# Six chain steps in place of four per block of projection products, in the last chunk of tokens

## The chip, the cores and the metric

The kernel runs on one core of a Trainium2 chip. The metric is the device time of one execution in microseconds (us); smaller is better. Before the change the median of three runs is 2636.89 us (2636.56 to 2642.58).

## The reference

One encoder layer over 2048 tokens of width 1024, all float32. Cut to what matters here:

```python
h = rmsnorm(x, norm1_g)
qa, ka, va, qm, km, vm, om, gm, mg = split_cols(h @ w_in, IN_SPLITS)
ya = windowed_gqa(qa, ka, va, ...)          # 8 heads, window of 128 to each side, softmax with a sink
ym = mlstm_branch(qm, km, vm, om, gm, ...)  # conv, a scan over the tokens forward and one backward, norm, gate om
g = sigmoid(mg + merge_b)
x = x + (g[:, :D] * (ya @ w_branch_attn) + g[:, D:] * (ym @ w_branch_mlstm)) @ w_out
x = x + hier_moe(rmsnorm(x, norm2_g), ...)  # 32 experts, two per token
```

## The kernel before, in words

Every float32 product is made as three products of a high and a low part (hi·hi, hi·lo, lo·hi), so each weight piece is split into `whi` (ACT, L236) and `wlo` (POOL or DVE, L239) after its load into `wraw` (SP, L220).

**First phase.** The tokens go in four chunks of 512 (0 to 3), each of four blocks of 128 tokens (the last chunk has blocks 12 to 15). For each chunk a list of pieces of `w_in` is worked off: keys, values and gates, then queries, the recurrence's inputs, its output gate `o`, and the eight merge pieces `mg`. All these products are line L319 on `hThi`/`hTlo`, called projection products here. A result of `mg` or `o` is drawn out of PSUM by ACT and stored (`mg_s` L912, `o_s`).

**Chains.** The other work of this phase is written as generators that are advanced a step at a time: attention of a block (`attn`: turned queries L505, scores L524/L525, their sum with the bias L527, maximum L529, `exp` L536, turned probabilities L545, product with the values L556, the turned reciprocal L572, result `yT` L578, stored to `ya_s` L579), the recurrence (`mhead`: L678 to L709, `mtile`: L732 to L765) and its closing part (`mpost_load`, `mpost`: gate load `og` from `o_s` L782, gate scaling L798, sum of the two directions L790, square and its sum L793/L795, root on POOL L197/L198, L800, L801, turning L805, copy L814, store to `ym_s` L815). `run_mms` issues the products of a group and after every 12 narrow or 6 wide ones (a block) takes `tick_n[0]` steps round robin over the chains. Up to the last chunk that is 2; in the last chunk, once the recurrence's inputs are all there (`qkv_done`), it is `TL`. The last chunk's queue of steps holds the forward recurrence to block 15, the attention of blocks 12 to 15, and the backward recurrence of blocks 15 to 12, pushed when `o` is through. A step that finds its chain empty is no step.

**Order.** The order in which the program writes the steps is not the order of the queues: outside the parts marked as a manual schedule, a list scheduler with its own timeline puts the instructions on the five engines' queues; each queue then runs strictly in its order. What the program writes earlier has the earlier place where several are ready.

**Second phase.** For chunks 3 down to 0: attention and recurrence results are loaded, multiplied by the branch weights (L319 on `yahi`, `yalo`, `ymhi`, `ymlo`: branch products), weighted (L1151 to L1156), multiplied by `w_out` (L319 on `uhi`, `ulo`, added to x in L1163), normed and routed, while the backward recurrence of the next chunk runs as a chain. For chunk 3 `yprep_first` does the loading, after all chains of the chunk are through: into `ulo` from `ya_s` and `ym_s` (SP, L1137), then `yahi`/`ymhi` by ACT (L1138), `yalo`/`ymlo` by DVE (L1139). `gprep` (turns L591, scan L605, L613, L614) prepares the gates of the next chunk's backward recurrence. **Third phase:** the experts, in a manual schedule.

Of the kernel before, what the change touches and what calls it, by code (L numbers as in the profile page):

```python
# [102 lines left out]
def body(tc, A, out, scr_ext=None, upto="all"):  # L103
    nc = tc.nc
    scr_ext = scr_ext or {}
    es = ExitStack()
    with es:
        pass
        _body(tc, nc, A, out, scr_ext, upto, es)


def _body(tc, nc, A, out, scr_ext, upto, es):
# [211 lines left out]
                ch.tick(tick_n[0])  # L324

    tick_n = [2]
    TL = 4


    Fes = ExitStack()  # L330
# [586 lines left out]
    def qkv_done(c):  # L917
# [4 lines left out]
        if c == NCH - 1:  # L922
            tick_n[0] = TL
        ch.drain("cv")
# [926 lines left out]
```

## Time and profile before

| | |
|---|---|
| median of the runs | 2636.89 us |
| profiled execution, own time | 2630.14 us |
| its span, first to last instruction | 2628.4 us |
| PE / DVE / ACT / POOL busy, share of the span | 94 / 61 / 49 / 35 % |
| last projection product ends at | 1210.24 us |
| first branch product starts at | 1236.36 us |
| first turn of the experts' inputs starts at | 1784.65 us |

PE is TensorE, PEld its weight loads, DVE VectorE, ACT ScalarE, POOL GpSimd, SP the queue that issues most transfers. Times in the trace count from the span's start. Matmuls overlap in the pipeline, so that a wide product lasts 0.40 us by the profile while the next starts 0.23 us after it.

### The profile page before, as it was taken

Reading aid. Unit: us, or ns where it says so; the run is one execution under the profiler, and the core shown is the slowest. Engines: PE = TensorE matmul, PEld = TensorE weight load, DVE = VectorE, ACT = ScalarE, POOL = GpSimd, SP = SyncE. Lnnn points to the kernel's source line nnn. Section 1 sums busy time; section 2 is a strip of 40 time slices with the busy share of each in tenths; the row PEclk is TensorE's granted clock in tenths of the full one; section 3 lists DMA queues with packets and bytes.
Section 4 is the critical chain, followed back from the end, with each engine's and each line's share of the span. In section 5 each row is a group of like instructions: output and inputs, shape, how many; then the busy total and the mean of one; then the engine's idle time right before and its main releaser. Section 6 shows DMA issues by size and latency. Waiting matters only on the chain. (4 is left out here: it accounts for less than half of the span.)

```text
span 2628.4 us, 39004 instructions
## 1 busy us (share of the span) xinstructions
PE 2474.8 (94%) x13932; PEld 2070.8 (79%) x13933; DVE 1613.8 (61%) x2687; ACT 1285.4 (49%) x2516; POOL 928.6 (35%) x918
## 2 busy tenths in 40 slices
PE   7999999999999999997898898988999999999997
PEld 7777987889778978875787887886777777777776
DVE  4454535544554655555858495767877676678765
ACT  4444545454544544443334242325766565667654
POOL 5443444334433433242544454532222111112111
PEclk9999999999999999998999998998999999999999
DMA  4534533453344534556777573639998797989974
GB/s 151 160 118 144 161 94 120 130 172 116 114 124 125 161 113 139 160 154 195 219 216 213 157 226 102 207 111 330 334 360 267 256 330 240 294 256 361 365 245 101
DMA packets 348411, 515.31 MB, mean 196 GB/s; under 512 B 25019, under 2 KB 212500, under 8 KB 348188
## 3 DMA queue, kind: packets, MB, share of 16 engines
q1 hardware_dynamic: 332140, 460.03, 53.4%
q0 software_dynamic: 14880, 48.20, 7.8%
q10 hardware_dynamic: 1168, 4.21, 0.4%
q8 instruction: 127, 2.08, 0.3%
q14 instruction: 96, 0.79, 0.1%
HBM read 420.83 MB, written 91.54 MB: 195 GB/s over the span
## 5 line engine op out<-in xcount | busy, mean ns | idle before, releaser
L239 POOL TENSOR_TENSOR wlo<-wraw,whi 128x512 fp32r<-128x512 f32 (+1 forms) x422 | 573.5, 1386 | 476.9 <-ACT whi L236 455.6
L1563 DVE TENSOR_TENSOR elo<-raw,ehi 128x1024 fp32r<-128x1024 f32 x256 | 299.4, 1220 | 26.3 <-ACT ehi L1562 26.3
L319 PE MATMUL mm<-hThi,whi 128*128 128x512 f32 x768 | 306.9, 400 | 0.0
L319 PE MATMUL mm<-hTlo,whi 128*128 128x512 f32 x768 | 304.4, 396 | 0.0
L319 PE MATMUL mm<-hThi,wlo 128*128 128x512 f32 x768 | 304.0, 396 | 0.0
L236 ACT ACTIVATE whi<-wraw 128x512 fp32r<-128x512 f32 (+1 forms) x424 | 233.4, 622 | 141.5 <-PE mm L319 67.5
L319 PE MATMUL mm<-whi,hThi 128*128 128x256 f32 (+1 forms) x896 | 261.2, 292 | 4.0 <-ACT ev L898 1.8
L1562 ACT ACTIVATE ehi<-raw 128x1024 fp32r<-128x1024 f32 x256 | 254.5, 1050 | 19.7 <-DMA raw<-w_expert_up 19.1
L319 PE MATMUL mm<-wlo,hThi 128*128 128x256 f32 (+1 forms) x896 | 256.9, 287 | 1.1 <-POOL wlo L239 1.1
L319 PE MATMUL mm<-whi,hTlo 128*128 128x256 f32 (+1 forms) x896 | 256.5, 286 | 0.0
L1677 POOL DMA_INDIRECT out<-y,idx x32 | 56.2, 1756 | 445.0 <-DVE y L1676 226.2
L1609 PE MATMUL mm<-ehi,xhi 128*128 128x512 f32 x512 | 205.2, 401 | 0.0
L1609 PE MATMUL mm<-ehi,xlo 128*128 128x512 f32 x512 | 200.7, 392 | 0.6 <-DVE xlo L1588 0.6
L319 PEld LDWEIGHTS mm<-whi,hThi 128*128 128x128 f32 x896 | 171.0, 191 | 8.1 <-ACT ev L898 2.1
L319 PEld LDWEIGHTS mm<-wlo,hThi 128*128 128x128 f32 x896 | 171.2, 191 | 3.4 <-issue 1.6
L319 PEld LDWEIGHTS mm<-whi,hTlo 128*128 128x128 f32 x896 | 171.0, 191 | 0.3 <-DVE hTlo L444 0.2
L319 PEld LDWEIGHTS mm<-hThi,wlo 128*128 128x128 f32 x768 | 144.3, 188 | 33.9 <-issue 3.2
L319 PEld LDWEIGHTS mm<-hThi,whi 128*128 128x128 f32 x768 | 144.6, 188 | 29.3
L319 PEld LDWEIGHTS mm<-hTlo,whi 128*128 128x128 f32 x768 | 144.5, 188 | 28.6
L319 PE MATMUL mm<-whi,uhi 128*128 128x256 f32 x448 | 134.0, 300 | 26.4 <-DVE x L1163 20.4
L1612 PE MATMUL mm<-elo,xhi 128*128 128x512 f32 x512 | 158.5, 391 | 0.0
L1563 DVE TENSOR_TENSOR elo<-rawd,ehi 128x1024 fp32r<-128x1024 f32 x128 | 151.5, 1221 | 10.9 <-ACT ehi L1562 10.4
(438 smaller groups left out, 5830.1 us busy)
## 6 DMA issues: line engine op xcount, KB each, us to landing
wraw<-w_in SPq DMA_DIRECT2D x152, 512.0 KB, 4.2
raw<-w_expert_gate SPq DMA_DIRECT2D x128, 512.0 KB, 9.2
raw<-w_expert_up SPq DMA_DIRECT2D x128, 512.0 KB, 10.4
rawd<-w_expert_down SPq DMA_DIRECT2D x64, 1024.0 KB, 11.5
mg_s<-evg SPq DMA_DIRECT2D x64, 256.0 KB, 3.1
gt<-mg_s SPq DMA_DIRECT2D x32, 512.0 KB, 6.0
wraw<-w_out SPq DMA_DIRECT2D x32, 512.0 KB, 6.2
xt<-x SPq DMA_DIRECT2D x16, 512.0 KB, 4.6
```

What stands on the lines that cost most here:

```text
L236: nc.scalar.activation(hi[:, ks, :W], r[:, k:k + 2, :W], AF.Copy)
L239: eng.tensor_sub(lo[:, ks, :W], r[:, k:k + 2, :W], hi[:, ks, :W].bitcast(F32))
L319: nc.tensor.matmul(o, l, r, start=st, stop=sp)
L1562: nc.scalar.activation(dst[0], src, AF.Copy)
L1563: nc.vector.tensor_tensor(dst[1], src, dst[0].bitcast(F32), op=OP.subtract)
L1609: nc.tensor.matmul(self.gu[h], x_[:, k % 4, :], self.wt(k)[0][:, h, :], start=k == 0 and i == 0, stop=False)
L1612: nc.tensor.matmul(self.gu[h], self.xs[k // 4][0][:, k % 4, :], self.wt(k)[1][:, h, :], start=False, stop=k == KT - 1)
L1677: nc.gpsimd.indirect_dma_start(out=out, out_offset=bass.IndirectOffsetOnAxis(ap=self.idx, axis=0), in_=y, in_offset=None, compute_op=OP.add)
```

## The change

One number: the steps that are taken after each block of the last chunk's products, from the point on where the recurrence's inputs are complete.

```diff
     tick_n = [2]
-    TL = 4
+    TL = 6
```

The steps themselves stay the same (some 260 of them are taken from that point to the end of the first phase in both). As written, they are through in the fourth merge piece before and in the second now. The scheduler turns this into other queue orders from there on, up to the third phase.

PE's queue where the first phase ends. Before, this is all that stands between the last projection product and the first branch product (T, O and rb belong to the attention of block 15, mw and mib to the recurrence of blocks 13 and 12, LF, gz and mrow to `gprep`):

```order
L545 MATMUL T<-ident,sc 128x128 x2
L805 MATMUL m<-ident,mw 128x128 x4
L545 MATMUL T<-ident,sc 128x128 x2
L758 MATMUL m<-mv_11210,mib 128x129 x2
L545 MATMUL T<-ident,sc 128x128 x4
L758 MATMUL m<-mv_11210,mib 128x129 x2
L572 MATMUL T<-ident,rb 128x128 x4
L556 MATMUL O<-PT,vv 64x512 x2
L805 MATMUL m<-ident,mw 128x128 x4
L591 MATMUL m<-ident,LF 4x128 x4
L591 MATMUL m<-ident,gz 4x128 x4
L613 MATMUL m<-ident,mrow 128x4 x4
```

Now the last projection product, what follows it, and the first branch products:

```order
L319 MATMUL mm<-hThi,wlo 128x512
L805 MATMUL m<-ident,mw 128x128 x4
L758 MATMUL m<-mv_11353,mib 128x129 x4
L805 MATMUL m<-ident,mw 128x128 x4
L591 MATMUL m<-ident,LF 4x128 x4
L591 MATMUL m<-ident,gz 4x128 x4
L613 MATMUL m<-ident,mrow 128x4 x4
L614 MATMUL m<-D_12126,ones_91 128x16
L678 MATMUL m<-ident,MM 128x128 x4
L319 MATMUL mm<-yahi,whi 128x512 x2
```

The eight turns of probabilities, the four turns of the reciprocal and the two rows of value products have moved ahead of the last 16 projection products; L614 and L678, which stood 20 and 36 branch products further on, have moved ahead of the first one.

DVE's queue at the gate scaling of block 12, before:

```order
L801 TENSOR_TENSOR mw<-mw,og 128x512
L527 TENSOR_TENSOR sc<-S,bias 128x256 x3
L529 TENSOR_REDUCE mx<-sc 128x4
L798 SCALAR_TENSOR_TENSOR og<-og,ogain 128x512
L531 TENSOR_TENSOR mx<-mx,sinkb 128x4
L748 TENSOR_TENSOR mdn<-mdn,EN 128x2
L532 TENSOR_SCALAR nmx<-mx 128x4
```

and now:

```order
L765 SCALAR_TENSOR_TENSOR Cst<-Cst,mil,m 128x129 x2
L801 TENSOR_TENSOR mw<-mw,og 128x512
L551 COPY PT<-T 128x512
L798 SCALAR_TENSOR_TENSOR og<-og,ogain 128x512
L748 TENSOR_TENSOR mdn<-mdn,EN 128x2
L749 RECIPROCAL mdn<-mdn 128x2
L750 TENSOR_TENSOR mw<-m,mdn 128x256
L578 TENSOR_TENSOR yT<-O,PT 128x512
```

The maximum of block 15's scores (L529 to L532) no longer straddles the gate scaling; it stands ahead of L801.

SP's queue at the loads of the branch inputs, before:

```order
L815 DMA ym_s<-hf 128x4x128
L220 DMA wraw<-w_branch_mlstm 128x4x256
L579 DMA ya_s<-yT 128x4x128
L220 DMA wraw<-w_branch_attn 64x4x256 x2
L1137 DMA ulo<-ya_s 128x4x128 x4
L1137 DMA ulo<-ym_s 128x4x128 x3
L1145 DMA gt<-mg_s 128x2x512
```

and now:

```order
L579 DMA ya_s<-yT 128x4x128
L656 DMA mw<-st_s 128x512
L658 DMA mv_12198<-v_s 128x4x128
L912 DMA mg_s<-evg 128x512
L815 DMA ym_s<-hf 128x4x128
L220 DMA wraw<-w_branch_mlstm 128x4x256
L782 DMA og<-o_s 128x512
L1137 DMA ulo<-ya_s 128x4x128 x3
L815 DMA ym_s<-hf 128x4x128
L1137 DMA ulo<-ya_s 128x4x128
```

The gate load for the next chunk (L782), which came after the loads of the branch inputs, now stands ahead of them, and one store of the closing part has come between them.

## Rows read from the trace of the kernel before

**Rows 1.** Busy time by stretches: stretch, length, PE, PEld, DVE, ACT, POOL, clock, DMA, GB/s.

```profile
1010.00:1020.00 10.00, 7.62 (x53) 7.42 (x52) 3.87 (x6) 2.29 (x5) 3.90 (x5) 0.83 0.73 231
...
1015.00:1195.00 180.00, 180.00 (x1042) 146.16 (x1042) 102.49 (x211) 86.68 (x229) 56.85 (x59) 1.00 0.50 154
...
1230.00:1240.00 10.00, 5.17 (x17) 3.60 (x18) 6.28 (x12) 4.79 (x8) 0.00 (x0) 0.50 1.16 310
...
1270.00:1280.00 10.00, 8.71 (x42) 6.85 (x40) 9.70 (x18) 2.48 (x5) 3.71 (x6) 1.00 1.01 333
```

**Rows 2.** PE's waits from 1195 to 1260 us: total, times, longest (us).

```profile
PE m L591 <- ACT hf L814: 4.5, 1, 4.5
PE T L572 <- DVE rb L568: 3.3, 1, 3.3
PE T L545 <- ACT sc L536: 3.1, 1, 3.1
PE m L805 <- DVE mw L801: 2.5, 1, 2.5
PE m L613 <- DVE mrow L605: 1.6, 1, 1.6
```

**Rows 3.** Timeline, PE: last projection product, first branch products (start, us, what).

```profile
1209.84 0.40 PE L319 MATMUL mm<-hThi,wlo 128*128 128x512 f32 x1
...
1236.36 1.22 PE L319 MATMUL mm<-yahi,whi 128*128 128x512 f32 x2
...
1237.38 0.63 PE L319 MATMUL mm<-yalo,whi 128*128 128x512 f32 x1
...
1241.97 0.40 PE L319 MATMUL mm<-yalo,whi 128*128 128x512 f32 x1
...
1242.20 0.39 PE L319 MATMUL mm<-yahi,wlo 128*128 128x512 f32 x1
```

**Rows 4.** Timeline, the closing part of blocks 13 and 12, and the loads.

```profile
1205.88 0.69 DVE L801 TENSOR_TENSOR mw<-mw,og 128x512 f32<-128x512 f32 x1
...
1211.59 0.69 DVE L798 SCALAR_TENSOR_TENSOR og<-og,ogain 128x512 f32<-128x512 f32 x1 [2.78 <-DMA og<-o_s]
...
1220.01 0.25 POOL L197 TENSOR_SCALAR mrs<-mss 128x4 f32<-128x4 f32 x1
...
1221.56 1.01 POOL L198 TENSOR_TENSOR mrs<-mrs,nhalf 128x4 f32<-128x4 f32 x1
...
1225.03 0.69 DVE L578 TENSOR_TENSOR yT<-O,PT 128x512 f32<-128x512 f32 x1 [4.82 <-issue]
...
1226.66 0.68 DVE L801 TENSOR_TENSOR mw<-mw,og 128x512 f32<-128x512 f32 x1
...
1227.56 2.48 SPq L1137 DMA_DIRECT2D ulo<-ya_s  x4
```

**Rows 5.** Timeline, PE: chain products among projection products, at the full clock.

```profile
1196.49 0.39 PE L734 MATMUL m<-Cst,mqk 128*128 128x129 f32 x2
...
1198.09 0.60 PE L805 MATMUL m<-ident,mw 128*128 128x128 f32 x4
...
1198.52 0.82 PE L545 MATMUL T<-ident,sc 128*128 128x128 f32 x6
...
1203.65 1.07 PE L556 MATMUL O<-PT,vv 128*64 128x512 f32 x2
```

**Rows 6.** PE's waits from 1236 to 1420 us: total, times, longest (us).

```profile
PE m L805 <- DVE mw L801: 3.4, 2, 1.8
PE mm L319 <- DVE x L1163: 2.8, 1, 2.8
PE m L805 <- DVE mw L750: 2.6, 1, 2.6
```

**Rows 7.** Waits from 900 to 1260 us, all engines: DVE for the gate load.

```profile
DVE og L798 <- DMA og<-o_s: 11.2, 4, 4.4
```

**Rows 8.** Timeline, PE: the one long wait among the last chunk's products.

```profile
1012.88 1.87 PE L691 MATMUL m<-mqk 128*128 128x128 f32 x8 [2.38 <-DMA mqk<-qk_s]
```

## The prediction, made before the changed kernel ran

> **What bounds the kernel now.** I read the busy time by stretches first, then PE's waits, then the timeline at the place where they pile up. In the last chunk's projections PE is taken up fully: 180.00 of 180 us from 1015 to 1195, at the full clock [rows 1]. The one long wait of that chunk, 2.38 us for a load of the recurrence [rows 8], lies ahead of the first place where the queues differ. So in the stretch where the steps are moved there is next to nothing to win: the steps are the same work, on a PE that is full with or without them.
>
> What can change is the seam behind it. The last projection product ends at 1210.24 and the first branch product starts at 1236.36 [rows 3]: 26.1 us, of which PE waits 15.0 in five pieces [rows 2] and spends the rest on chain products that come too late to lie beside anything, at a clock that falls to 0.50 [rows 1]. Read backwards, the seam ends with the branch inputs: the first branch product needs all four attention tiles of the chunk, their loads are issued from 1227.56 on [rows 4], and SP reaches them only after the store of the last attention tile, which waits for DVE's `yT` at 1225.03. DVE stood 4.82 us before it [rows 4], waiting for attention's late value products; behind `yT` the closing part of block 12 was held up too (its root was ready at 1222.57, its L801 ran at 1226.66).
>
> I sum against the profiled execution's own time, 2630.14 us; the median of the runs is 2636.89, 6.8 above it, and I take that offset to stay.
>
> **The change, part by part.**
>
> *Chain products moved ahead of the last projections.* Eight turns of probabilities, four turns of the reciprocal and two rows of value products (four matmuls) leave the seam. At the full clock six turns take 0.82, four larger ones 0.60, two value matmuls 1.07 [rows 5]: 1.1 + 0.6 + 2.1 = 3.8 us. They take these 3.8 us from PE in the projections, since PE is full there, so the move itself is worth 0; the seam with the same work left in it is 26.1 - 3.8 = 22.3 us.
>
> Here a rule of the Trainium skill speaks otherwise. From 1015 to 1195 the weight loads are busy 146.16 of 180 us while PE shows 180.00 [rows 1]. "Perfetto Trace Analysis", section "Identifying the Most-Contended Engine", says that busy time of matmuls is a poor measure of how full TensorE is and that the weight loads' share should be used. By it PE would have 19% of room there, and the 3.8 us would vanish beside the projections. The rows speak against that: products start 0.23 us apart without a gap (1241.97 and 1242.20 [rows 3]), and a value product holds the next one back by its own half microsecond [rows 5]. I price the move at 0 and keep the other reading as a rival.
>
> *The seam after the change.* I follow the new queues from the last projection product. (a) Block 13's L801 stands on DVE right behind two state updates, and PE's second output product of block 12 waits for the latter. After that product PE still has four output products (about 0.45, by 0.39 for two), four value matmuls (2.1) and 16 projection products (16 x 0.23 = 3.7): 6.3 us. From the end of block 13's L801 to the end of block 12's gate scaling L798 it took 1206.57 to 1212.28, 5.7 us [rows 4], nearly all of it the round trip of the gate load. So L798 ends about when the last projection product does. (b) Then DVE has ten queue rows to L795, against 15 before. From L798's end to the root's start was 7.7 us with other work between; the four 128x512 operations alone are 4 x 0.69 = 2.8. I take 4.5, nearer to the lower end, because attention's reciprocal and copies are gone from between. (c) The root on POOL, with one split between its halves in both orders: 1220.01 to 1222.57, 2.6. (d) L800 and L801: 1.4, no longer held up by `yT`. So block 12's L801 ends 8.5 us after the last projection product, against 17.1 before. (e) SP now has the next chunk's gate load ahead of the branch inputs; it needs the tile that this L801 frees. That is the new wait, and the loads stand behind it: one issue of about 0.6 (2.48 for four [rows 4]), so the first load goes out at about 9.2. (f) From there to the first branch product it took 1227.56 to 1236.36, 8.8; the store slipped between adds about what the scan's wait at the end takes away. The seam is then 18.0 us, against 22.3: **4.3 us** gained. Bounds: with (a) 2 us earlier and (b) at 2.8, 14.3 and 8.0 gained; with (a) 2 us later and (b) at 7.7, 23.2 and 0.9 lost. The clock is as low after 18 us as after 26: 13 branch products take 5.6 us where 3.0 would do, before and after.
>
> *The first chunk of the second phase.* L614 and L678 now stand ahead of all branch products, so DVE does the head of block 11 (some 3 us, four wide operations) in the seam, where it waits, and not from 1250 on, where it is busy 9.70 of 10 [rows 1]. PE waits for DVE in this chunk 3.4 + 2.8 + 2.6 = 8.8 us [rows 6]. Ends 0 and 8.8; I take **2.0**, nearer to nothing, since DVE's total stays and 0.3 us in 10 is all the slack it has.
>
> *The middle.* New queue orders on a full PE can bring a wait where there was none. Nearest rows: none for 180 us, or one as in rows 8, 2.38 us plus the clock that it cost (0.83 in its stretch, at most 1.7 us), 4.1. I take **0.5** lost, nearer to none. Later chunks and the experts keep their patterns and are costed at 0: they start earlier by what the seam gives.
>
> Sum: -4.3 - 2.0 + 0.5 = **-5.8 us**: 2624.3 against the own time, 2631.1 as a median.
>
> **The rivals.**
>
> *The seam closes to the recurrence's own path* and the waits of rows 6 go as well: 8.0 + 6 = 14 us gained, 2623. For it: every late item of rows 2 but the scan hangs on attention's tail or on DVE behind it. Against: the gate load is a round trip that nothing in the new order shortens, and it now stands before the branch loads.
>
> *The products moved find room beside the projections*: 5.8 + 3.8 = 9.6 gained, 2627.3. This is what the page on trace analysis would lead to; 0.23 us from product to product speaks against it.
>
> *Nothing is left*: the chains are bound by their own latency, the scheduler can place few steps earlier, and the new wait on SP eats what DVE gives: 2637. For it: as written, the steps are through two pieces earlier, yet in the new queues attention's last value products still stand only 16 products before the end, 3.7 us.
>
> *Slower*: DVE held by the gate loads reaches PE. DVE has stood up to 4.4 us at L798, 11.2 in all [rows 7], without PE's noticing. With the chains denser, score sums and copies of attention stand behind such a wait, and a score or turn product whose input is late holds all projection products queued behind it. Place: from the first six-step block to the seam. Price: 4.1 us each, as above. Two eat the gain; from the fourth on (16.4 - 5.8 = 10.6 lost, 2647.5) it is slower by over 0.3%. There are four such gate loads. Against it: between scores and turns 5 us or more of products remain in the new queue.
>
> **How the numbers follow.** What a measurement of this kernel can tell from no change is 0.3%, 7.9 us. My forecast has 0.45, with its own range from 1 to 10 us gained, so about 0.10 of it is faster by more than that. The closed seam has 0.22, the room beside the projections 0.05, nothing left 0.14, slower 0.14. Faster by over 0.3%: 0.10 + 0.22 + 0.04 = 0.36; slower: 0.13; within: 0.51. The range reaches from the closed seam with a little more (17 gained, 2620) to most of the slower case (7 lost, 2644); outside it I leave the full four waits and a seam that gives still more.
>
> **What would show it.** Right: the seam, from the last projection product to the first branch product, at about 18 us with the attention's value products ahead of it, the gate load issued before the loads into `ulo`, and PE without a wait of 2 us between 1015 and the seam. The last projection product should end about 3.8 us later, near 1214. The first chunk's waits for DVE should be below 8.8 us. Wrong: a seam under 15 us (the branch loads waited for less than I think), or one of 22 and more (the gate load decides); a last projection product at 1218 or later (waits in the middle); or an equal seam and a time moved by the later chunks, which I cost at nothing.

## The result, and the profile after

The changed kernel takes 2617.88 us (median of 5 runs, 2614.93 to 2624.0) against 2636.56 (median of 5, 2635.47 to 2642.58): a ratio of 0.9933, with a 95% interval from 0.9912 to 0.9955. That is 18.7 us between the medians; 5.8 were forecast, and the range ended at 17. The two profiled executions differ by less: spans of 2628.4 and 2616.0 us, 12.4. So two things are to be explained, a gain in the profile twice as large as forecast, and 6 us that the medians differ beyond it.

I cut the two profiled executions at the same places of the program: the first turn of the recurrence that waits for a load [rows 8], the end of the last projection product, the first branch product [rows 3], the first branch product of the next chunk, the start of the experts and the end.

| stretch | before, us | after, us | difference | forecast |
|---|---|---|---|---|
| up to the turn of rows 8 | 1012.88 | 1011.92 | -0.96 | 0 |
| to the last projection product | 197.36 | 198.07 | +0.7 | +3.8 and +0.5 |
| seam | 26.1 | 16.3 | -9.8 | -8.1 |
| first chunk of the second phase | 127.8 | 121.7 | -6.1 | -2.0 |
| the three other chunks | 420.5 | 422.4 | +1.9 | 0 |
| experts to the last PE row | 832.3 | 834.1 | +1.9 | 0 |

PE's waits from 1000 to 1250 us, changed kernel (total, times, longest), which answer to [rows 2] and [rows 8]:

```profile
PE m L805 <- DVE mw L801: 4.0, 1, 4.0
PE mm L319 <- ACT yahi L1138: 1.8, 1, 1.8
PE m L691 <- DMA mqk<-qk_s: 1.7, 1, 1.7
PE m L613 <- DVE mrow L605: 1.4, 1, 1.4
PE mm L319 <- ACT mdn L741: 1.3, 1, 1.3
```

The three waits for attention's tail of [rows 2] (turns, reciprocal, and the copy behind the closing part) are gone. What is left is block 12's closing part, the head of block 11 and the branch inputs. The timeline of the seam, changed kernel, in order of time:

```profile
1199.72 0.69 DVE L801 TENSOR_TENSOR mw<-mw,og 128x512 f32<-128x512 f32 x1
...
1204.78 0.69 DVE L798 SCALAR_TENSOR_TENSOR og<-og,ogain 128x512 f32<-128x512 f32 x1 [3.77 <-DMA og<-o_s]
...
1209.15 0.69 DVE L795 TENSOR_REDUCE mss<-hf 128x4 f32<-128x512 f32 x1
...
1209.60 0.39 PE L319 MATMUL mm<-hThi,wlo 128*128 128x512 f32 x1
...
1210.00 0.19 POOL L197 TENSOR_SCALAR mrs<-mss 128x4 f32<-128x4 f32 x1 [11.12 <-DVE mss L795]
...
1211.79 1.02 POOL L198 TENSOR_TENSOR mrs<-mrs,nhalf 128x4 f32<-128x4 f32 x1
...
1212.77 4.62 POOL L239 TENSOR_TENSOR wlo<-wraw,whi 128x512 fp32r<-128x512 f32 x3
...
1212.86 1.73 DVE L800 TENSOR_TENSOR mw<-mw,mrs 128x512 f32<-128x512 f32 x1
1214.62 1.64 DVE L801 TENSOR_TENSOR mw<-mw,og 128x512 f32<-128x512 f32 x1
...
1216.28 0.33 SPq L782 DMA_DIRECT2D og<-o_s  x1
1216.67 1.53 SPq L1137 DMA_DIRECT2D ulo<-ya_s  x3
...
1221.91 0.63 ACT L1138 ACTIVATE yahi<-ulo 128x512 fp32r<-128x512 f32 x1 [3.85 <-DMA ulo<-ya_s]
...
1226.33 1.22 PE L319 MATMUL mm<-yahi,whi 128*128 128x512 f32 x2 [1.82 <-ACT yahi L1138]
```

Against [rows 4]: block 13's L801 ends 9.6 us ahead of the last projection product (3.7 before), the gate scaling L798 4.5 us ahead of it, the root starts right at its end, and the branch loads leave 6.7 us behind it (17.3 before).

### The profile page after: what moved, and what is told of

Its sections match the earlier page's. It is cut to its first block, busy times and chain, and to the rows that moved or that the text cites. A ratio compares the mean times of both kernels' runs of the same rounds, so it can differ in the third digit from the quotient of the medians.

```text
span 2616.0 us, 39004 instructions
## 1 busy us (share of the span) xinstructions
PE 2470.0 (94%) x13932; PEld 2071.6 (79%) x13933; DVE 1602.5 (61%) x2687; ACT 1284.5 (49%) x2516; POOL 930.3 (36%) x918
## 5 line engine op out<-in xcount | busy, mean ns | idle before, releaser
L826 DVE SCALAR_TENSOR_TENSOR cacc<-cstg,colv,cacc 128x512 f32<-128x512 f32 x128 | 110.9, 867 | 76.0 <-ACT cacc L823 73.6
```

The lines of the kernel that those rows point to most:

```text
L826: nc.vector.scalar_tensor_tensor(acc, stg[:, r:r + CH], colv[:, j, r:r + 1], acc, op0=OP.mult, op1=OP.add)
```

## The experiments

All compare with the kernel before, run beside them. Seams and stretches are those of the profiled runs.

**1. Attention's extra steps alone.** Eight or twelve steps for all chains give the same queues as six; so do six steps that last only until the projections `o` are through, while six from there on give those of before. What matters is that attention's last steps are written ahead of the backward recurrence, which begins at `o`.

```diff
-                ch.tick(tick_n[0])
+                ch.tick(tick_n[0]); [ch.step(m) for m in more]
...
-            tick_n[0] = TL
+            tick_n[0] = TL; more.extend(["att", "att"])
```

> Four steps of every chain per block, and two more of the attention chain alone; the recurrence chains keep four. All queues then hold the same rows in the same order as with the change. Theory A (what counts is that attention's last steps are written ahead of the backward recurrence): 0.993 of the time before, some 2618 us, with a seam of 16 to 17 us, as with the change. Theory B (the recurrence's extra steps carry part of it, by something other than the order of the queues): less than half of the gain, 2628 us or more. Should it come out over 2624, the change's own gain was partly spread between runs.

Measured: 2620.35 us, ratio 0.995 (0.993 to 0.9969); seam 16.45 us, first chunk 123.9. Theory A holds: the recurrence's extra steps add nothing. This is at the same time a second sample of the change, and it gains 13 us, not 18.

**2. The recurrence's extra steps alone** (`more.extend(["mh", "ml", "mp"])`).

> The opposite: one more step per block of each of the three recurrence chains, attention keeps four. Scores, eight turns and four value products of attention then stand behind the last projection product on PE. Theory A (attention's tail decides the seam): no gain, 0 to 8 us slower than before, 2637 to 2645 us; seam 27 us or more. Rival (any steps that are written earlier shorten the seam): 3 to 9 us faster than before, 2628 to 2634 us.

Measured: 2630.6 us, 0.9985 (0.9971 to 0.9998). The first branch product, its wait, and the loads behind attention's last store, in this kernel's timeline:

```profile
1223.83 0.37 SPq L579 DMA_DIRECT2D ya_s<-yT  x1
...
1225.33 4.04 SPq L1137 DMA_DIRECT2D ulo<-ya_s  x4
...
1235.54 1.22 PE L319 MATMUL mm<-yahi,whi 128*128 128x512 f32 x2 [2.77 <-ACT yahi L1138]
```

The last projection product ends at 1199.96, so the seam is 35.6 us, as A has it. A's price was off: what attention leaves in the seam is missing in the stretch ahead of it (188.6 us against 197.4), and both together are as long as before (224.2 and 223.5). The time is 4 us lower, near the limit of what can be told, and not higher: it lies in the range that I gave the rival, though the seam didn't shorten. Where these 4 us come from stays open.

**3. Before, with shorter waits for the gate loads.**

```diff
-        og = mix.tile([P, 512], F32, name="og")
+        og = fp.tile([P, CH + 4], F32, name="cstg", bufs=2)[:, :512] if t in (12, 14) else mix.tile([P, 512], F32, name="og")
```

> The kernel before, where the gate tiles of blocks 14 and 12 lie in the conv's staging buffers, free by then, so that no gate load waits for the block ahead of it and DVE isn't held by its round trip. PE's queue is the same up to the first branch product. Theory A (the seam before hangs on attention's tail; the gate's round trip lies beside it): 0 to 2 us gained, 2635 to 2637 us, seam 25 to 26 us. Rival (DVE's hold of 4 us at the gate scaling makes attention's copies and block 12's closing part late): seam 22 us, 2632 us.

Measured: 2631.31 us, 0.9985 (0.9972 to 0.9999); seam 21.6 us. Its timeline:

```profile
1208.51 0.69 DVE L798 SCALAR_TENSOR_TENSOR og<-og,ogain 128x512 f32<-128x512 f32 x1 [1.43 <-DMA og<-o_s]
...
1218.45 0.69 DVE L578 TENSOR_TENSOR yT<-O,PT 128x512 f32<-128x512 f32 x1 [2.67 <-ACT PT L575]
...
1220.99 2.25 SPq L1137 DMA_DIRECT2D ulo<-ya_s  x4
```

Theory A falls here, the rival's seam and time come out: with DVE's holds for gate loads cut from 11.2 us in all [rows 7] to 7.3, attention's last `yT` starts 9.9 us after the last projection product instead of 14.8 [rows 3, 4], and the seam is 4.5 us shorter. In the kernel before, the last steps of attention's score maximum (L531, L532) stood behind the gate scaling on DVE, and its sums behind those. The change takes attention out from behind it.

The hold itself is the smaller part of these 4.9 us. DVE's L565, PE's turns and value products, and the busy time with the granted clock (columns as in [rows 1]), in the kernel before and then in this one:

```profile
1216.22 1.23 DVE L565 TENSOR_TENSOR den<-den,esink 128x8 f32<-128x8 f32 x1
...
1220.26 1.11 PE L572 MATMUL T<-ident,rb 128*128 128x128 f32 x4 [3.29 <-DVE rb L568]
1221.31 3.63 PE L556 MATMUL O<-PT,vv 128*64 128x512 f32 x4
...
1215.00:1220.00 5.00, 1.98 (x9) 1.43 (x7) 4.91 (x10) 3.45 (x7) 3.92 (x4) 0.50 0.62 188
```

```profile
1212.93 0.16 DVE L565 TENSOR_TENSOR den<-den,esink 128x8 f32<-128x8 f32 x1
...
1215.84 0.66 PE L572 MATMUL T<-ident,rb 128*128 128x128 f32 x4 [2.66 <-DVE rb L568]
1216.43 1.93 PE L556 MATMUL O<-PT,vv 128*64 128x512 f32 x4
...
1213.00:1218.00 5.00, 2.34 (x10) 0.89 (x8) 2.79 (x8) 2.82 (x6) 4.83 (x6) 1.00 0.77 225
```

The end of L798 comes 1.4 us earlier against the last projection product (0.6 us behind it in place of 2.0), DVE's work from there to the reciprocal's copy takes 1.3 us less, most of it L565, and PE's turns and value products 2.2 us less, at a granted clock of 1.00 in place of 0.50. That the clock stayed up because PE's waits were shorter is likely (its first one in the seam is 1.64 us here and 3.07 before), but not tried by itself.

**4. The change, block 11's gate load off SP's path** (the same edit for block 12 alone; block 11's load then goes out early, PE's queue being the same up to the first branch product).

> The changed kernel, where block 12's gate tile lies in a conv staging buffer. Block 11's gate load then needs no tile of block 12 and goes out ahead, so SP has no gate load between the stores and the branch loads; PE's queue is the same up to the first branch product. Theory A (the new wait on SP is on the path, 1.5 us of wait and 0.4 of issue): first branch load 1.5 to 1.9 us earlier after the last projection product, seam 14.5 us, 1 to 2 us faster than the change, 2616 us. Rival 1 (the first branch product waits for the closing part of block 12, not for the loads): seam 16.3 us as with the change, 2618 us. Rival 2 (the earlier loads crowd others out): seam 17 us and more.

Measured: 2621.59 us, 0.9949 (0.993 to 0.9967); seam 16.5 us. Its timeline:

```profile
1219.18 0.64 SPq L220 DMA_DIRECT2D wraw<-w_branch_mlstm  x1
1219.87 1.82 SPq L1137 DMA_DIRECT2D ulo<-ya_s  x3
...
1227.12 1.34 ACT L1138 ACTIVATE yahi<-ulo 128x512 fp32r<-128x512 f32 x2 [4.01 <-DMA ulo<-ya_s]
```

The loads left 4.8 us after the last projection product (ended 1215.06) in place of 6.7, and the first landed 12.1 us after it in place of 11.9. From the weight load's issue to the first input it is 7.9 us here and 7.8 in the change (1214.11 to 1221.91). The wait that I had put on SP's path is hidden beside the transfers. Rival 1's time is right, and its reason isn't settled here. The first branch product waits for the fourth of these loads, and on SP that one stands behind the store of block 12's result. The fourth load and its input, in the change and in this kernel:

```profile
1219.42 1.35 SPq L1137 DMA_DIRECT2D ulo<-ya_s  x1
...
1225.65 0.63 ACT L1138 ACTIVATE yahi<-ulo 128x512 fp32r<-128x512 f32 x1 [1.26 <-DMA ulo<-ya_s]
```

```profile
1224.90 1.06 SPq L1137 DMA_DIRECT2D ulo<-ya_s  x1
...
1230.93 0.63 ACT L1138 ACTIVATE yahi<-ulo 128x512 fp32r<-128x512 f32 x1 [1.41 <-DMA ulo<-ya_s]
```

Against the last projection product the load leaves at 9.4 and 9.8 us, its input is there at 15.7 and 15.9, and block 12's copy (L814) ends at 8.1 in both. So this run can't tell the closing part from the transfers; experiment 11, which takes the store out from between the loads, can.

**5. The change, gate tiles of blocks 13 and 12 both moved** (`t in (12, 13)`).

> The changed kernel with the gate tiles of blocks 13 and 12 in the conv's staging buffers: neither the gate load of block 12 nor that of block 11 waits for the closing part ahead of it, and DVE loses its hold of 3.8 us at the gate scaling of block 12. PE's queue is the same up to the first branch product. Theory A (block 12's closing part bounds the seam, and the hold delays it): last root of block 12 and everything behind it up to 3 us earlier, seam 13 to 14.5 us, 2 to 3 us faster than the change, 2617 to 2619 us at a before of 2636. Theory B (the branch loads' transfers bound it: in the run with block 12's tile alone they left 1.9 us earlier and landed as late as before): seam 16 to 16.6 us, no faster than that run, 2621 us.

Measured: 2620.97 us against 2638.57, 0.9937 (0.9924 to 0.9951); seam 16.0 us. DVE in this kernel's timeline:

```profile
1205.90 0.16 DVE L748 TENSOR_TENSOR mdn<-mdn,EN 128x2 f32<-128x2 f32 x1 [2.00 <-ACT mdn L741]
...
1209.91 0.42 DVE L750 TENSOR_TENSOR mw<-m,mdn 128x256 f32<-128x256 f32 x1
...
1211.83 0.69 DVE L795 TENSOR_REDUCE mss<-hf 128x4 f32<-128x512 f32 x1
```

No gate scaling stands there now, and DVE waits for ACT's L741 instead, which waits for PE's output products (L734). L795 ends 0.4 us ahead of the last projection product (1212.89); in the change it is 0.2. So the closing part hangs on the place of block 12's last output product, 16 projection products ahead of the end, and not on the gate load. Theory B's time is right. Since the closing part kept its place, the run doesn't test whether that part bounds the seam.

**6. Turns of probabilities twice** in the last chunk.

```diff
-                for h in range(4):
+                for h in list(range(4)) * (2 if t >= NT - TPC else 1):
                     nc.tensor.transpose(p[:, h, :], sc[:, h, i * P:(i + 1) * P], ident)
```

> The changed kernel, where each group of four turns of probabilities of the last chunk's attention is done twice into the same tile: 22 groups, 88 turns more (of 0.096 us each by the time from one to the next, 8.5 us). Theory A (PE is full in the projections, so products moved there take their own time, and the change's gain is not free room): the stretch up to the last projection product is 6 to 9 us longer, and the time 6 to 9 us longer than the change's. Rival (the products find room beside the projections): the stretch is at most 3 us longer.

Measured: 2637.18 us, 0.9997 (0.9986 to 1.0008), by the ratios 12 to 17 us over the change; the stretch from the turn of rows 8 is 212.7 us. Turns in the stretch, by tile, of the change and of this kernel:

```profile
L545 PE MATMUL T<-ident,sc x88: 270/272/273, 1030.7 to 1199.3; 128*128 128x128 f32 x88
```

```profile
L545 PE MATMUL T<-ident,sc x176: 270/273/273, 1031.6 to 1215.0; 128*128 128x128 f32 x176
```

That is 13.1 us over the comparable runs of the change (199.6, below), more than the turns' own 8.5, and stretch and time are both over A's 6 to 9 us. Part of the excess is other work: by count in the trace, 12 more chain products than in the change (eight of L758, four of L805) stand in this stretch. The rival falls: there is no room beside the projections.

**7 and 8. Two buffers for the routing entries**, in the change and in the kernel before: `ent` and `si` of the routing step with `bufs=2`.

> The changed kernel with two buffers in place of one for the routing entries and their slots, so that DVE's copy of the next entries need not wait until the eight serial slot stores of the chunk before are done. All queues but DVE's keep their order. Theory C (the 6.7 us that the change's lead loses in chunk 2's output products are this wait: PE stands 10.6 us there): the wait goes, 5 to 9 us faster than the change, 2612 to 2616 us at a before of 2636. Rival (the stores themselves, on POOL, hold what comes next): within 2 us of the change.

> The kernel before with the same two buffers for the routing entries. Theory C: the kernel before has this wait in chunks 2 and 1 (PE stands 8.35 and 7.86 us); both go, 8 to 16 us faster than before, 2620 to 2628 us, and then the change's lead over it is 8 to 12 us, the seam and the first chunk alone. Rival: within 2 us of before.

Measured: 2617.94 us, 0.9921 (0.9906 to 0.9936), and 2633.53, 0.9982 (0.9971 to 0.9994). The kernel before gains 5 us, which neither theory C (8 to 16) nor the rival (up to 2) gave. Of DVE's two waits for the slot stores one was left in each, 12.1 us. Inconclusive, so with three:

**9 and 10. Three buffers** (`bufs=3`).

> The changed kernel with three buffers for the routing entries and their slots; with two, one of the two waits of DVE for the slot stores was left (12.1 us). All queues but DVE's keep their order. Theory C (the later chunks' give and take between the two kernels is this wait): no wait for the stores is left and PE's wait of 10.6 us at the first router turn of chunk 2 goes; 5 to 9 us faster than the change, 2613 to 2617 us at a before of 2637. Rival (the roots on POOL stand behind the serial stores, and the wait only changes its name): PE waits 8 us or more at the same place, within 2 us of the change.

> The kernel before with the same three buffers. Theory C: both waits of DVE for the slot stores go, 5 to 12 us faster than before, 2625 to 2632 us; the change's lead over this kernel is then that of seam and first chunk, 9 to 13 us. Rival: within 2 us of before.

Measured: 2612.05 us against 2636.7, 0.9907 (0.9886 to 0.9927), and 2630.14, 0.9978 (0.9962 to 0.9993). DVE's waits from 1226 to 1770 us in the change, then in the change with three buffers:

```profile
DVE h L1213 <- POOL rs L198: 20.9, 10, 4.6
DVE ent L1308 <- DMA slot_s<-ent,si: 19.6, 2, 13.5
```

```profile
DVE h L1213 <- POOL rs L198: 41.3, 12, 11.4
```

The wait goes, and on DVE as much comes back under another name (20.4 us more for 19.6 less): the roots on POOL stand behind the serial stores. PE's wait of 10.6 us is gone. Both kernels gain, the change 7 to 11 us by the ratios (0.9907 against 0.9933 and 0.995) and the kernel before 6. The lead stays, at 18 us, which is more than the 9 to 13 of theory C. The profiled pair has 17.2; 4.4 of it lie ahead of the turn of rows 8, where the change can't act, 8.6 in the seam and 4.8 in the first chunk.

The three later chunks are equal on balance in this pair (417.5 and 416.1 us), as forecast. But theory C's reason for it fails: one chunk's loss of 7.2 us and the next one's gain of 6.5 in the change were to be this wait falling differently, and without the wait two chunks together are still 10.0 us slower than in the kernel before, and the last one 8.6 faster. The change with three buffers is faster than both kernels.

**11. The gate ahead of the root** in the closing part of the change.

```diff
-        nc.vector.tensor_mul(h_, h_, rs[:, :, None].to_broadcast([P, 4, P]))
         nc.vector.tensor_tensor(h_, h_, og.rearrange("p (h d) -> p h d", h=4), op=OP.mult)
+        nc.vector.tensor_mul(h_, h_, rs[:, :, None].to_broadcast([P, 4, P]))
```

> The changed kernel, where the closing part multiplies by the gate first and by the root after it, so that one multiplication of DVE instead of two stands behind the root. The queues change: block 12's last multiplication now stands on DVE behind the first branch input's second part, and block 11's head comes behind the first branch product on PE. Theory A (block 12's closing part and block 11's head bound the seam): seam 12 to 14 us, 2 to 4 us faster than the change, 2618 us at a before of 2637. Theory B (the branch loads' transfers bound it): the first input lands some 12 us after the last projection product as with the change, seam 15.5 to 17 us, time as with the change.

Measured: 2637.35 us, 1.0001 (0.9989 to 1.0014); seam 15.9 us, first input 11.5 us after the last projection product (1208.16). All four loads leave ahead of block 12's store here, and the seam is no more than 0.5 us shorter: B is right about the seam. But the time is that of the kernel before. PE in this kernel:

```profile
1221.81 1.09 PE L805 MATMUL m<-ident,mw 128*128 128x128 f32 x4 [11.34 <-DVE mw L801]
1222.69 1.06 PE L591 MATMUL m<-ident,LF 128*4 128x128 f32 x4
1224.01 1.22 PE L319 MATMUL mm<-yahi,whi 128*128 128x512 f32 x2 [0.26 <-ACT yahi L1138]
```

Between these and the branch products there is no head of block 11 any more (L613, L614, L678 come after). The first chunk then takes 132.0 us, 10 more than in the change. Busy time of the first chunk by engine, three kernels (before, change, this one):

```profile
sum 127.80, PE 115.31 PEld 103.20 DVE 86.85 ACT 42.10 POOL 55.09; mean PE 28.83 PEld 25.80 DVE 21.71 ACT 10.53 POOL 13.77
```

```profile
sum 121.70, PE 111.71 PEld 100.17 DVE 79.96 ACT 41.92 POOL 54.44; mean PE 27.93 PEld 25.04 DVE 19.99 ACT 10.48 POOL 13.61
```

```profile
sum 132.00, PE 118.90 PEld 106.62 DVE 86.32 ACT 42.07 POOL 54.02; mean PE 29.73 PEld 26.65 DVE 21.58 ACT 10.52 POOL 13.51
```

With the head in the seam DVE is busy 6.9 us less in this chunk; with the head back behind it, 86.32 again. But PE's own busy time is 7.2 us longer than in the change, and the granted clock of the chunk differs: 0.95 before, 0.98 in the change, 0.91 here. The kernel before with two buffers, whose PE queue is that of before, also had 0.91 and took 131.7 us. Other orders changed too, so this run points to the head's place but doesn't isolate it.

**12. Three buffers and the gate ahead of the root.**

> Both of these edits in the changed kernel. By theories A and C their gains add up: 7 to 13 us faster than the change, 2609 to 2615 us at a before of 2637. By B and C: as the run with three buffers. By the rivals: as the change.

Measured: 2631.41 us, 0.9983 (0.9969 to 0.9996). None of the three forecasts came: the loss of experiment 11 stays, and the three buffers take 5 us off it.

## Why the prediction was wrong

**Direction, and the mechanism of the seam,** hold: it closes because attention's tail no longer stands in it, PE waits nowhere for 2 us between 1015 and the seam, later chunks and experts count for nothing on balance. The sizes don't. Three steps failed: the first chunk at 2.0 us (6.1 measured in the change, 3.9 at equal clock), the moved products and the middle at 4.3 us of cost (2.4 measured), and the offset of 6.8 us between profile and median (0 in the change). The sign of a last projection product near 1214 failed with the second: it ended at 1210.0.

**"The move itself is worth 0"**, or 3.8 us more in the stretch ahead, and 0.5 for the middle: too much by about 2. The stretch from the turn of rows 8 fell into two classes by the clock granted there (last section). At equal clock: 199.6 us in four runs of the change's order (199.63, 199.59, 199.64, 199.68) against 197.2 to 197.4 in three of before's (197.36, 197.21, 197.21); 198.1 in two against 195.0 in one. So the moved products cost 2.2 to 3.1 us; the 195.0 is that of experiment 3, where the gate tiles differ too. I take 2.4. "Worth 0" set the same length at both places, but in the seam these 16 products took 6.6 us, at a clock that fell to 0.50. That the profile of the change shows only 0.7 is due to the clock, which stayed up there and had fallen in the profile of before (0.83 in [rows 1]).

The reading by which they cost nothing falls with experiment 6. The Trainium skill ("Perfetto Trace Analysis", section "Identifying the Most-Contended Engine") would read room from the weight loads' 146 of 180 us; here the trace doesn't agree: 88 more turns and the 12 products that came with them took 13 us.

**The seam**, 18.0 us by my steps and 16.3 measured, comes near in its sum only by luck, because errors offset. Step (a) put the end of L798 at the end of the last projection product; it is 4.5 us ahead of it, since the denser chains bring block 13's L801 forward by 6 us. Step (b) let the closing part follow L798, and 4.5 us it did take, so the root starts 4.5 us earlier than I had it. But experiment 5 shows that L798 is worth no more than 0.2 us on this path: PE's last output product is what it hangs on. Step (c) is 2.8 against 2.6. Step (d) is 3.4 against 1.4: L800 and L801 take 1.73 and 1.64 us, not 0.69. Step (e), the new wait on SP, exists (1.5 us), and experiment 4 shows that the seam is no shorter without it; the loads leave at 6.7 in place of 9.2. Step (f) is 9.7 against 8.8, with the transfers as its length. Net, 1.7 us.

**"Ends 0 and 8.8; I take 2.0, nearer to nothing, since DVE's total stays"**: this term was mis-sized most. It measured 6.1 us in the change and 3.9 in the first experiment; the pairs with two and three buffers have 7.9 and 4.8. The clock goes with the difference: the chunk had 0.98 in the change, 0.95 in the first experiment and 0.95 before, so I take 3.9 as the value at equal clock. DVE was the engine waited for there [rows 1, 6], and PE's waits for it in the change are 5.5 us, below 8.8 as the sign had it. The head itself was priced about right: the nine rows of DVE that left the chunk are 3.5 us long (2.6 in the first experiment), and the rest of the 6.9 us by which DVE is less busy is the same rows running shorter. What failed is the discount. That the total stays is no argument when the work moves from where DVE is full to where it waits. That the head's place gives these 3.9 us is argued, not shown: in experiments 4 and 5 the same nine rows left, DVE's busy time fell by only 2.4 and 1.6 us, and the chunk still took no more than 123.6 and 124.7.

At equal clock the parts add to -9.8 - 3.9 + 2.4 = -11.3 us; the profiled pair, with its clocks, has -12.4. That is nearest to the first rival, "the seam closes and the waits of rows 6 go as well", which I gave 0.22; my point against it, the gate load in front of the branch loads, is what experiments 4 and 5 speak against: without it the seam was 16.5 and 16.0. The gate loads' rival on the slower side never came up: in the change DVE's longest hold for one, 3.77 us ahead of the seam, made PE wait nowhere among the projections.

**The offset.** "6.8 above it, and I take that offset to stay" failed: the profiled execution of before (2630.14) lies at the lower end of its own runs, which went from 2628 to 2645 in 23 runs beside experiments 1 to 4, and that of the change (2617.88) at its median. The repeat in experiment 1 has 13 us, with an interval of 8 to 18; the first comparison 18, with 12 to 23. 12.4 lies in both. The two pairs with the same buffers on either side give 16 and 18. Whether the true gain is nearer to 12 or to 18 stays open; the traces account for 11 to 12, and what the medians have beyond that has no cause shown here.

## What to carry to other kernels

Two chains that end in the same seam are not to be priced by their own latency alone: look at what stands behind each in-order wait, because a late load in one chain (here DVE held up to 4 us for a gate) delays the other, and reordering the two takes that away without a shorter load. Look also at what the wait sets off: here a hold shorter by 1.4 us came with 4.9 us at the end of the chain. Work that moves off an engine's busy stretch into its idle one isn't to be priced near nothing because the engine's total stays; here some 3 us of it came with 3.9 or more. And where a sum is made against one profiled execution, see first where that lies among the kernel's runs: here this alone was as large as the forecast.

## What the runs showed of the hardware

**DVE beside POOL.** Block 12's two last multiplications took 1.73 and 1.64 us while POOL ran three weight splits from 1212.77, and 0.69 each in experiment 3, where no split ran beside them. The splits were slower too, 4.62 us for three against 1.27 for one in experiment 3 that ran while DVE stood idle. The Trainium skill ("SBUF — State Buffer", section "Summary: rules for kernel authors") says that a DVE instruction with two SBUF inputs and a GpSimd one that reads SBUF exclude each other, the later one waiting until the first is done. The durations agree: each seems to wait for one of the other. It wasn't tried to take the splits away.

**A clock that falls in one run and not in the next.** The wait for a load of [rows 8] was 1.5 to 2.6 us long in the 14 profiled runs, also between kernels with equal queues (1.72 in the change, 1.96 in experiment 1). Behind 1.90 us and more the clock fell in nine runs of ten (not behind 2.06 in experiment 3), behind the four waits of 1.47 to 1.72, the change's among them, it didn't. Windows from 1010 to 1030 of the change, then of experiment 1, whose queues are the same (columns as in [rows 1]):

```profile
1010.00:1030.00 20.00, 18.28 (x154) 18.08 (x153) 12.08 (x23) 10.53 (x31) 8.79 (x9) 1.00 0.74 226
```

```profile
1010.00:1030.00 20.00, 18.28 (x140) 18.29 (x141) 11.89 (x23) 8.85 (x26) 8.66 (x8) 0.91 0.65 197
```

The one stayed at 2.4 GHz throughout, the other spent part of the stretch at 1.2 GHz, and from there to the last projection product they took 198.1 and 199.6 us. Over whole runs the time goes with the clock only roughly: of the 23 runs of before beside experiments 1 to 4, the five with a mean clock of 0.975 took 2638.7 us on average, the two with 0.979 took 2632.8, but the seven with 0.976 took 2634.2.
